# A two-layer transformer trunk with its own list scheduler: larger planned latencies for transfers and for TensorE's inputs, and all hi/lo splits on VectorE

## The chip, the cores and the metric

One NeuronCore of a Trainium2 chip runs the program alone. The metric is the device time of one execution in microseconds (us). Engine names are those of the profile: PE is TensorE's matmul row and PEld its weight loads, DVE is VectorE, ACT is ScalarE, POOL is GpSimd, and SP is SyncE, whose queue issues the DMAs.

## The reference, cut to what matters

The input is 512 tokens of 1024 float32 values. Two layers follow each other, and each has an attention part and a gated ConvFFN, both between an RMSNorm before and an RMSNorm after:

```python
for layer in range(2):
    if layer == 0:                        # stick-breaking attention
        a = rmsnorm(h, sb_pre_g[0])
        q, k, v = split(a @ sb_w_qkv[0], 3)
        o = stick_breaking_attention(q, k, v)       # 16 heads of 64
        h = h + rmsnorm(merge(o) @ sb_w_o[0], sb_post_g[0])
    else:                                 # forgetting attention
        kvf = rmsnorm(h, kv_norm_g) @ w_kvf         # keys, values, forget gates
        q = rmsnorm(h, fox_pre_g[0]) @ fox_w_q[0]
        o = forgetting_attention(q, k, v, fcum)
        h = h + rmsnorm(merge(o) @ fox_w_o[0], fox_post_g[0])
    hdn = causal_conv3(rmsnorm(h, ffn_pre_g[layer]) @ w_up[layer]) + conv_b
    gate, up = split(hdn, 2)              # 2816 columns each
    h = h + rmsnorm((gelu(gate) * up) @ w_down[layer], ffn_post_g[layer])
```

## The kernel before, in words

**Split operands.** Nearly every float32 matrix product is done with operands split in two: `hi` is the value rounded to the type that TensorE reads at full rate, and `lo` is what is left over. A product is then three matmuls, hi by hi, hi by lo and lo by hi. The activations are kept as `AH` and `AL` (hi and lo, 128 partitions by 8 by 512).

**Weights.** `stream` lists 196 weight tiles of 512 KB in the order of their use. `make` issues the transfer of a tile into `raw` (two buffers), casts it to `whi` on ACT (L389; with a per-row gain L382) and computes `wlo = raw - whi`, in two halves of 128x512 on the engine that the tile names (L393; with a gain L383, on DVE). `whi` and `wlo` have eight buffers each (`NW`). A `raw` buffer is free for the tile after next once both halves of `wlo` are done. The tile names DVE except for the rows 1, 5 and 7 of the two output projections (`sb_w_o`, `fox_w_o`), which name POOL (`POOL_ROWS`, L417 and L432).

**The phases.** "pre" loads and normalises the input and transposes small tables (tiles `crow` and `grow`, in two buffers, through PE at L885); tiles of a later phase reuse the memory of an earlier one, so the first write of the attention phase waits for the last use in "pre". Then come the attention of layer 0 (about 46 to 250 us of the span), its output projection and FFN (to about 660 us), and the same for layer 1. A head (`Attn.head`) is a chain over four engines: scores on PE (L643), exponentials on ACT and scans, masks and products on DVE (L653 to L681), transposes on PE (L689), a hi/lo split on ACT and DVE (L695, L696), the product with the values on PE (L701), and the merge (L710, L711). The projections of the next heads (L445 for q and k, L623 for v) and, late in the phase, the first output-projection matmuls (L743) stand between as work that PE can do while a head waits. At the end of `Attn.run` the attention's output is split too: `AH` by a cast on ACT (L730) and `AL` by a subtraction (L731), for the head pairs 0 to 3 on POOL and for 4 to 7 on DVE.

**The order is planned.** The class `Order` takes all instructions, works out who depends on whom, and simulates them at build time with costs written in the code (`cost`, `schedule`). At each step an engine takes, of the instructions whose inputs the plan says are there, the one of the lowest rank: the rank is the program position, plus 300 for weight casts and splits (`BEHIND`), less 150 for work that empties PSUM (`AHEAD`). The order that results is fixed for PE, DVE, ACT and POOL; SP's queue is not fixed by it. At run time the engines follow this order and wait at semaphores for true readiness. The plan's latencies decide only which instruction stands ahead of which. Of a transfer the plan holds that it lands `LEAD` + size/`BYTES` + `LAND` after its issue, 1300 + 1691 + 700 ns for 512 KB when the wire is free, and each result reaches another engine `HOP` = 60 ns after its end.

Of the kernel before, what the change touches and what calls it, by code (L numbers as in the profile page):

```python
# [18 lines left out]
KT = D // P  # L19
# [10 lines left out]
EARLY = 3  # L30
BEHIND = 300
AHEAD = 150
POOL_ROWS = (1, 5, 7)
FILL = (4, 5)
SCALE = HD**-0.5

# [4 lines left out]
def f32(ap):  # L41
    return ap.bitcast(F32)


class Order:
# [4 lines left out]

    GRAIN = 64
    SKIPPED = ("Drain", "EventSemaphore", "UnconditionalBranch", "TilePoolBoundary", "RegisterMove", "ISA", "Call")
    ISSUE, LEAD, LAND, BYTES = 520, 1300, 700, 310.0
    HOP = 60

    def __init__(self, tc, phases):
        self.tc, self.nc, self.phases = tc, tc.nc, phases
# [182 lines left out]
    def schedule(self, prog, preds):  # L240
        N = len(prog)
        rank = [n + self.shift.get(i.name, 0) - (AHEAD if self.evicts(i) else 0) for n, i in enumerate(prog)]
        eng = [self.engine(i) for i in prog]
        cost = [self.cost(i) for i in prog]
        succ = [[] for _ in range(N)]
        left = [len(d) for d in preds]
        for n, d in enumerate(preds):
            for m, k in d.items():
                succ[m].append((n, k))
        free = {e: 0.0 for e in sorted(set(eng))}  # L250
        now = {e: [] for e in free}
        later = {e: [] for e in free}
        at, start, wire = [0.0] * N, [0.0] * N, 0.0
        for n in range(N):
            if not left[n]:
                heapq.heappush(later[eng[n]], (0.0, n))
        for _ in range(N):
            best = None
            for e in free:
                if now[e]:  # L260
                    c = (free[e], e)
                elif later[e]:
                    c = (max(free[e], later[e][0][0]), e)
                else:
                    continue
                best = c if best is None else min(best, c)
            t, e = best
            while later[e] and later[e][0][0] <= t:
                m = heapq.heappop(later[e])[1]
                heapq.heappush(now[e], (rank[m], m))  # L270
            n = heapq.heappop(now[e])[1]
            hold, done = cost[n]
            start[n], free[e], end = t, t + hold, t + done
            if str(prog[n].opcode) == "DMACopy":
                wire = max(wire, t + self.LEAD) + done
                end = wire + self.LAND
            for m, k in succ[n]:
                at[m] = max(at[m], t if k == 2 else free[e] if eng[m] == e else end + self.HOP)
                left[m] -= 1
                if not left[m]:  # L280
                    heapq.heappush(later[eng[m]], (at[m], m))
        return start
# [3 lines left out]
def tile_trunk(  # L286
# [22 lines left out]
    nc = tc.nc  # L309
# [53 lines left out]
    stream = []  # L363
# [6 lines left out]
    def row_tile(w, k, eng=nc.vector):  # L370
        return (w[k * P : (k + 1) * P, :].rearrange("(a p) c -> p a c", p=P), 1, D, None, eng)
# [39 lines left out]
    for g in range(4):  # L411
        for pr in range(2):
# [1 line left out]
            qk = [col_tile(wq, c0), col_tile(wk, c0)]  # L414
            v = [col_tile(wv, g * 256, 256, 4 * j, 4) for j in range(2)]
            stream += qk if pr else qk + v if g else v + qk
    stream += [row_tile(sb_w_o[0], k, nc.gpsimd if k in POOL_ROWS else nc.vector) for k in range(KT)]  # L417

    def ffn_stream(l):
        s = []  # L420
        for c in range(NC):
            s += [col_tile(w_up[l], c * P), col_tile(w_up[l], FF + c * P)]
        return s + [row_tile(w_down[l], k) for k in range(NC)]

    stream += ffn_stream(0)
    for g in range(4):
        for pr in range(2):
# [1 line left out]
            qk = [col_tile(fox_w_q[0], c0, g=KT), col_tile(w_kvf, c0, g=0)]  # L429
            v = [col_tile(w_kvf, D + g * 256, 256, 4 * j, 4, g=0) for j in range(2)]  # L430
            stream += qk if pr else qk + v if g else v + qk
    stream += [row_tile(fox_w_o[0], k, nc.gpsimd if k in POOL_ROWS else nc.vector) for k in range(KT)]  # L432
    stream += ffn_stream(1)


# [69 lines left out]
    class Attn:  # L505
# [208 lines left out]
        def run(self):  # L714
            self.project_v(0, PAIRS)
            if self.fox:
                self.gates()
                self.project(0, 2, (PAIRS[1] + 1, PAIRS[2] + 1))
                self.gate_keys(0)
            else:  # L720
                self.project(0, 2, (PAIRS[0] + 1, PAIRS[1] + 1))
            for p in range(NPAIR):
                self.head(p, 0)
                if p + 1 < NPAIR:
                    self.project(p + 1)
                end = self.head(p, 1)
                if p % 2 and p + 1 < NPAIR:
                    self.project_v((p + 1) // 2)
            for p in range(NPAIR):
                nc.scalar.copy(AH[:, p, :], self.oT[:, p, :])  # L730
                (nc.gpsimd if p < 4 else nc.vector).tensor_tensor(  # L731
                    out=AL[:, p, :], in0=self.oT[:, p, :], in1=f32(AH[:, p, :]), op=ALU.subtract
                )
            return end
# [128 lines left out]
    with tc.tile_pool(name="pre", bufs=2) as pool:  # L863
# [13 lines left out]
        for l in range(2):  # L877
            rows = [conv_w[l, w].rearrange("(c p) -> c p", p=P) for w in range(3)]
            rows.append(conv_b[l].rearrange("(c p) -> c p", p=P))
            for i in range(2):  # L880
                t = pool.tile([2 * nb, P], F32, name="crow")
# [5 lines left out]
        t = pool.tile([2 * KT, P], F32, name="grow")  # L887
# [5 lines left out]
        t = pool.tile([P, NH], F32, name="bf")  # L893
# [14 lines left out]
    with tc.tile_pool(name="attn0", bufs=2) as pool:  # L908
        pool = order.pool(pool, "attn0", 2)
        act_table("natural_log_exp_and_others")  # L910
        end = Attn(pool, False).run()
# [3 lines left out]
    with tc.tile_pool(name="attn1", bufs=2) as pool:  # L915
        pool = order.pool(pool, "attn1", 2)
        act_table("natural_log_exp_and_others")
        end = Attn(pool, True).run()
# [28 lines left out]
```

## Time and profile before

| what | value |
|---|---|
| median of three runs | 1273.48 us (1272.51 to 1274.8) |
| the profiled execution | 1276.16 us |
| its span, first to last instruction | 1274.3 us |
| mean granted TensorE clock | 0.996 of full speed |
| busy | PE 97%, DVE 64%, ACT 51%, POOL 8% |

The profiled execution is one execution; its span leaves out 1.9 us at the two ends. PE's busy time counts a matmul's pipeline latency, so that a row of matmuls that each wait a little can still look busy.

### The profile page before, as it was taken

Reading aid. Unit: us, or ns where it says so; the run is one execution under the profiler, and the core shown is the slowest. Engines: PE = TensorE matmul, PEld = TensorE weight load, DVE = VectorE, ACT = ScalarE, POOL = GpSimd, SP = SyncE. Lnnn points to the kernel's source line nnn. Section 1 sums busy time; section 2 is a strip of 40 time slices with the busy share of each in tenths; the row PEclk is TensorE's granted clock in tenths of the full one; section 3 lists DMA queues with packets and bytes.
Section 4 is the critical chain, followed back from the end, with each engine's and each line's share of the span. In section 5 each row is a group of like instructions: output and inputs, shape, how many; then the busy total and the mean of one; then the engine's idle time right before and its main releaser. Section 6 shows DMA issues by size and latency. Waiting matters only on the chain.

```text
span 1274.3 us, 16774 instructions
## 1 busy us (share of the span) xinstructions
PE 1236.5 (97%) x6485; PEld 1054.5 (83%) x6485; DVE 815.1 (64%) x1304; ACT 650.8 (51%) x1085; POOL 101.0 (8%) x163
## 2 busy tenths in 40 slices
PE   6999999899999999999998999989999999999998
PEld 6788897689888888888897988867898888888886
DVE  5699989677655555433477988784675555554323
ACT  4678777555433333323577888774454333333221
POOL 2000003120000000000101221342100000000001
PEclk9999999999999999999999999999999999999999
DMA  5322221125433333333221122221443333333311
GB/s 188 108 75 83 68 67 50 50 83 149 114 92 93 98 100 99 100 96 90 63 78 41 50 65 69 65 85 50 121 144 100 100 99 99 94 93 96 99 33 66
DMA packets 145927, 111.97 MB, mean 88 GB/s; under 512 B 4680, under 2 KB 136120, under 8 KB 145848
## 3 DMA queue, kind: packets, MB, share of 16 engines
q1 hardware_dynamic: 145848, 110.90, 29.4%
q8 instruction: 51, 0.84, 0.3%
q14 instruction: 28, 0.23, 0.1%
HBM read 108.79 MB, written 2.10 MB: 87 GB/s over the span
## 4 chain that ended last, share of the span: by engine, by line
PE 80%; DVE 12%; ACT 3%; DMA 2%; POOL 1%; issue 1%; SPq 0%; DVEq 0%; POOLq 0%; ACTq 0%
PE PS L445 47%; PE PS L743 20%; PE PS L623 5%; PE PS L701 3%; PE PS L643 2%; DVE ec L679 2%; PE PS L689 2%; DVE wlo L393 1%; DVE ec L681 1%; DVE PL L696 1%; PE PS L466 1%; DVE t L463 1%; DMA H<-x_dram 1%; DVE H L477 1%; DVE QS L594 1%
## 5 line engine op out<-in xcount | busy, mean ns | idle before, releaser
L445 PE MATMUL PS<-AH,whi 128*128 128x512 f32 (+1 forms) x1088 | 398.7, 366 | 3.4 <-DVE QS L594 3.4
L445 PE MATMUL PS<-AL,whi 128*128 128x512 f32 (+1 forms) x1088 | 398.6, 366 | 0.0
L445 PE MATMUL PS<-AH,wlo 128*128 128x512 f32 (+1 forms) x1088 | 398.5, 366 | 0.0
L393 DVE TENSOR_TENSOR wlo<-raw,whi 128x512 fp32r<-128x512 f32 x332 | 219.0, 698 | 197.3 <-ACT whi L389 196.8
L389 ACT CAST whi<-raw 128x1024 fp32r<-128x1024 f32 x172 | 180.6, 1050 | 196.5 <-PE PS L445 171.8
L445 PEld LDWEIGHTS PS<-AH,whi 128*128 128x128 f32 x1088 | 206.1, 189 | 35.2 <-DVE QS L594 3.7
L445 PEld LDWEIGHTS PS<-AL,whi 128*128 128x128 f32 x1088 | 206.2, 190 | 31.7
L445 PEld LDWEIGHTS PS<-AH,wlo 128*128 128x128 f32 x1088 | 206.0, 189 | 31.8
L821 DVE SCALAR_TENSOR_TENSOR hc<-PS,cw,hc 128x511 f32<-128x511 f32 (+1 forms) x176 | 131.3, 746 | 5.9 <-ACT hc L819 2.9
L743 PE MATMUL PS<-whi,ah 128*128 128x512 f32 x352 | 109.2, 390 | 0.0
L743 PE MATMUL PS<-whi,al 128*128 128x512 f32 x352 | 109.1, 389 | 0.0
L743 PE MATMUL PS<-wlo,ah 128*128 128x512 f32 x352 | 109.0, 389 | 0.0
L844 DVE TENSOR_TENSOR al<-act,ah 128x512 fp32r<-128x512 f32 x44 | 30.3, 691 | 116.6 <-ACT ah L843 116.6
L843 ACT CAST ah<-act 128x512 fp32r<-128x512 f32 x44 | 27.4, 623 | 145.0 <-PE PS L743 138.1
L743 PEld LDWEIGHTS PS<-whi,al 128*128 128x128 f32 x352 | 66.1, 188 | 13.7
L743 PEld LDWEIGHTS PS<-wlo,ah 128*128 128x128 f32 x352 | 66.1, 188 | 13.7
L743 PEld LDWEIGHTS PS<-whi,ah 128*128 128x128 f32 x352 | 65.9, 188 | 13.6
L623 PE MATMUL PS<-whi,AH 128*128 128x256 f32 x256 | 73.9, 289 | 0.0
L623 PE MATMUL PS<-wlo,AH 128*128 128x256 f32 x256 | 73.6, 288 | 0.0
L623 PE MATMUL PS<-whi,AL 128*128 128x256 f32 x256 | 73.3, 287 | 0.0
L826 ACT ACTIVATE hc<-hc 128x512 f32<-128x512 f32 x44 | 27.8, 631 | 85.0 <-DVE hc L821 85.0
L451 POOL TENSOR_SCALAR ss<-ss 128x1 f32<-128x1 f32 x31 | 9.8, 315 | 771.1 <-ACT junk L474 720.1
(132 smaller groups left out, 1770.6 us busy)
## 6 DMA issues: line engine op xcount, KB each, us to landing
raw<-w_up_dram SPq DMA_DIRECT2D x88, 512.0 KB, 3.8
raw<-w_down_dram SPq DMA_DIRECT2D x44, 512.0 KB, 3.6
raw<-sb_w_qkv_dram SPq DMA_DIRECT2D x24, 512.0 KB, 3.8
raw<-w_kvf_dram SPq DMA_DIRECT2D x16, 512.0 KB, 3.7
raw<-sb_w_o_dram SPq DMA_DIRECT2D x8, 512.0 KB, 3.6
raw<-fox_w_q_dram SPq DMA_DIRECT2D x8, 512.0 KB, 3.7
raw<-fox_w_o_dram SPq DMA_DIRECT2D x8, 512.0 KB, 3.7
H<-x_dram SPq DMA_DIRECT2D x4, 512.0 KB, 8.3
```

The costliest lines, as they stand in the source:

```text
L389: order.move(nc.scalar.copy(hi, raw), BEHIND)
L393: order.move(eng.tensor_tensor(out=fl[:, s], in0=fr[:, s], in1=fh[:, s], op=ALU.subtract), BEHIND)
L445: nc.tensor.matmul(ps, a[:, k, :m], b[:, k, t0:t1], start=i == 0, stop=i == n - 1)
L623: nc.tensor.matmul(ps[:, o], a[:, k, sl], m[:, k % 4, :], start=i == 0, stop=i == 3 * KT - 1)
L643: nc.tensor.matmul(z[:, ZOFF[b] : ZOFF[b] + n], a[:, b * P : (b + 1) * P], m[:, :n], start=i == 0, stop=i == len(passes) - 1,)
L679: nc.vector.tensor_tensor_scan(C[:, ::-1], self.R[:, ::-1], C[:, ::-1], 0.0, ALU.mult, ALU.add)
L701: mm = nc.tensor.matmul(av[:, j * P :], V[:, j, hh, :], m[:, o : o + n], start=i == 0, stop=i == 7,)
L743: nc.tensor.matmul(y[:, c, :], s[:, sl], m[:, 0, c * 512 : (c + 1) * 512], start=k == 0 and i == 0, stop=k == n - 1 and i == 2,)
L821: nc.vector.scalar_tensor_tensor(out=hc[:, s:], in0=y[:, i, : T - s], scalar=col[:, 2 - s : 3 - s], in1=hc[:, s:], op0=ALU.mult, op1=ALU.add,)
L826: nc.scalar.activation(hs[0], hs[0], AF.Gelu_apprx_tanh)
L843: nc.scalar.copy(ah, act[:, k, :])
L844: nc.vector.tensor_tensor(out=al, in0=act[:, k, :], in1=f32(ah), op=ALU.subtract)
```

## The change

Three edits. `LAND`, the last part of a transfer's planned latency, goes from 700 to 2700 ns. `HOP` becomes 350 ns where the instruction that receives the result is one of PE, and stays at 60 ns for the other engines. And POOL loses its splits: the rows 1, 5 and 7 of both output projections (12 halves of 128x512) and `AL` of the head pairs 0 to 3 in both layers (8 subtractions of 128x512) go to DVE, as the other rows and pairs already did.

```diff
-POOL_ROWS = (1, 5, 7)
...
-    ISSUE, LEAD, LAND, BYTES = 520, 1300, 700, 310.0
-    HOP = 60
+    ISSUE, LEAD, LAND, BYTES = 520, 1300, 2700, 310.0
+
+    HOP = {"PE": 350}
...
             for m, k in succ[n]:
-                at[m] = max(at[m], t if k == 2 else free[e] if eng[m] == e else end + self.HOP)
+                at[m] = max(at[m], t if k == 2 else free[e] if eng[m] == e else end + self.HOP.get(eng[m], 60))
...
-    stream += [row_tile(sb_w_o[0], k, nc.gpsimd if k in POOL_ROWS else nc.vector) for k in range(KT)]
+    stream += [row_tile(sb_w_o[0], k) for k in range(KT)]
...
-    stream += [row_tile(fox_w_o[0], k, nc.gpsimd if k in POOL_ROWS else nc.vector) for k in range(KT)]
+    stream += [row_tile(fox_w_o[0], k) for k in range(KT)]
...
                 nc.scalar.copy(AH[:, p, :], self.oT[:, p, :])
-                (nc.gpsimd if p < 4 else nc.vector).tensor_tensor(
+                nc.vector.tensor_tensor(
                     out=AL[:, p, :], in0=self.oT[:, p, :], in1=f32(AH[:, p, :]), op=ALU.subtract
                 )
```

## Rows read from the trace of the kernel before

**Rows 1.** Busy time, share of the span and instructions of each engine.
```profile
PE 1236.5 (97%) x6485; PEld 1054.5 (83%) x6485; DVE 815.1 (64%) x1304; ACT 650.8 (51%) x1085; POOL 101.0 (8%) x163
```

**Rows 2.** Windows: length; busy of PE, PEld, DVE, ACT, POOL; PEclk; DMA share; GB/s.
```profile
0.00:46.00 46.00, 33.53 (x240) 31.66 (x241) 26.48 (x56) 21.62 (x33) 8.11 (x22) 1.00 0.53 165
46.00:186.00 140.00, 139.27 (x822) 121.37 (x821) 130.26 (x170) 106.02 (x142) 2.55 (x2) 0.99 0.27 80
186.00:250.00 64.00, 57.21 (x304) 46.12 (x303) 53.34 (x63) 42.67 (x61) 12.15 (x8) 1.00 0.12 39
...
276.00:660.00 384.00, 384.00 (x1920) 327.47 (x1919) 211.86 (x337) 161.96 (x244) 7.51 (x20) 1.00 0.34 98
...
830.00:880.00 50.00, 44.16 (x219) 34.66 (x219) 31.84 (x58) 31.63 (x67) 19.40 (x22) 1.00 0.24 75
```

**Rows 3.** Waits of the whole run: us in total, times, longest.
```profile
ACT whi L389 <- DMA raw<-w_up_dram: 16.5, 14, 3.1
...
ACT whi L389 <- DMA raw<-sb_w_qkv_dram: 5.7, 4, 3.1
...
PE PS L701 <- DVE PL L696: 3.1, 5, 1.4
...
PE PS L689 <- POOL ec L669: 2.3, 4, 1.0
...
PE PS L689 <- DVE ec L681: 1.9, 2, 1.2
```

**Rows 4.** Instructions that ran on POOL at L393.
```profile
L393 POOL TENSOR_TENSOR wlo<-raw,whi 128x512 fp32r<-128x512 f32 x12 | 15.9, 1346 | 205.5 <-ACT whi L389 205.5
```

**Rows 5.** Chain that ended last, 186 to 250 us: start, us, what.
```profile
196.25 1.66 DVE ec L653
197.91 1.29 DVE ec L655
...
204.41 2.75 DVE wlo L393 x2
...
219.51 0.56 DVE ec L653
220.07 0.20 DVE ec L655
220.27 0.60 DVE AL L731
...
246.57 2.52 POOL wlo L393 x2
```

**Rows 6.** POOL's timeline in the same stretch.
```profile
196.19 2.84 POOL L393 TENSOR_TENSOR wlo<-raw,whi 128x512 fp32r<-128x512 f32 x2 [33.26 <-ACT whi L389]
```

**Rows 7.** The same chain, 828 to 882 us.
```profile
848.39 1.13 DVE ec L669
...
850.93 2.26 DVE wlo L393 x2
...
856.90 0.49 DVE ec L669
```

**Rows 8.** The same chain, 24 to 60 us.
```profile
24.53 2.87 DMA crow<-conv_w_dram
...
34.64 1.20 DVE wlo L393 x2
...
36.70 6.57 DMA raw<-sb_w_qkv_dram
43.29 1.04 ACT whi L389
...
50.95 6.91 PE PS L445 x30
```

**Rows 9.** DMA issues: KB each, median us from issue to landing.
```profile
raw<-w_up_dram SPq DMA_DIRECT2D x88, 512.0 KB, 3.8
```

**Rows 10.** Windows around the first heads, columns as in Rows 2.
```profile
40.00:46.30 6.30, 4.03 (x23) 3.07 (x21) 3.20 (x5) 2.35 (x4) 0.00 (x0) 1.00 0.34 104
46.30:49.70 3.40, 3.31 (x9) 2.63 (x9) 1.91 (x4) 2.11 (x3) 0.00 (x0) 0.50 0.48 154
```

## The prediction

> **What bounds the kernel now.** I read the busy times first: PE is busy 97% of the span and no other engine more than 64% [rows 1], so only what lies between PE's matmuls can be won. The windows by stage say where that is [rows 2]. In the FFN of layer 0 (276 to 660 us) PE is busy all 384.00 of 384 us: an edit that acts there alone is worth nothing. PE's idle time sits at the start (46.00 - 33.53 = 12.5 us) and in the last heads of the two attention phases, 64.00 - 57.21 = 6.8 us in one and 50.00 - 44.16 = 5.8 us in the other. The same rows give the second engine to watch: DVE is busy 130.26 of 140 us in most of the first attention phase and 53.34 of 64 us at its end, but only 31.84 of 50 us at the end of the second.
>
> The waits come next [rows 3]. ACT stands 16.5 us for transfers of `w_up`, all of it under the FFNs, where PE does not notice; 5.7 us for `sb_w_qkv`, at the start. PE's own waits for a head's results are short: 3.1 + 2.3 + 1.9 = 7.3 us in 11 waits. Last I read the chain that ended last, in the stretches with idle PE. In 186 to 250 us it goes mostly through DVE, and some of its DVE steps are far longer than the same step elsewhere [rows 5]: L653 takes 1.66 us and later 0.56, L655 1.29 and later 0.20, two halves of `wlo` 2.75 us where the two at 34.64 took 1.20 [rows 8]. POOL was subtracting `wlo` when L653 and L655 were slow, from 196.19 for 2.84 us [rows 6].
>
> **The change, part by part.**
>
> *Splits from POOL to DVE.* Gone are 12 halves on POOL [rows 4] and 8 subtractions for `AL`, four a layer. What they cost on the chain: 1.66 - 0.56 = 1.10, 1.29 - 0.20 = 1.09 and 2.75 - 1.20 = 1.55 us of slowed DVE work, and the last pair of halves that PE's first output block waits for, 2.52 us on POOL where DVE has 1.20: 1.32 us. That is 5.06 us in layer 0 [rows 5, 8]. In layer 1 it is 1.13 - 0.49 = 0.64 and 2.26 - 1.20 = 1.06, together 1.70 us [rows 7]. So 6.8 us can be given back. Added on DVE are 20 instructions; half of a pair is 0.60 us [rows 8], and one `AL` was 0.60 us [rows 5]. The pair at 246.57 is already netted, so 18 x 0.60 = 10.8 us are new. Their cover is DVE's idle time, 64.00 - 53.34 = 10.7 us and 50.00 - 31.84 = 18.2 us [rows 2]; queued behind each new split is the next step of a head, and PE's transposes or value products behind that. Splits have the lowest priority in the plan, so I expect them in gaps, but an instruction that has begun is finished: I let a bit under half of their time, 4.5 us, reach the chain. Net: 4.5 - 6.8 = -2.3 us. Bounds: -6.8 us (all in gaps) and 10.8 - 6.8 = +4.0 us (none).
>
> One rule speaks against this edit. DVE is the busier engine by the rows, 815.1 us against POOL's 101.0 [rows 1]. The Trainium skill, "Perfetto Trace Analysis", section "Optimizing Scalar/DVE Operations", says that when DVE is saturated, handing some elementwise work to GpSimd may make sense, and adds that the two share a read port, so it might not help. By its first half this part of the sum would be the +4.0, by its second half the -6.8; the slow L653 beside POOL's `wlo` agrees with the second.
>
> *`HOP` 350 for PE.* The plan now thinks that each result reaches PE 290 ns later, so PE takes another ready matmul first, and at run time the result is there when its turn comes. What it can save is bounded by the 7.3 us of waits in 11 places [rows 3]. 11 x 0.29 = 3.2 us would go if each were shortened by the margin and a filler stood ready; late in a phase fillers run out, so I take -2.5 us. The price is a filler ahead of a result that was in time: 6.91 / 30 = 0.23 us for an L445 matmul [rows 8]. A head enters PE three times (scores, transposes, value products). If, an estimate, the last four heads of each layer have no slack and every entry is hit, that is 2 x 4 x 3 x 0.23 = 5.5 us. Bounds: -7.3 us (all waits gone) and +5.5 us.
>
> *`LAND` 2700.* The plan's old latency for 512 KB, 3.69 us, is close to the measured median of 3.8 [rows 9]. With 5.69 us the casts stand later in ACT's order. In the FFNs this removes some of the 16.5 us and moves nothing, since PE is full. It matters at the start. There a transfer took 6.57 us (36.70 to 43.27), ACT then cast it for 1.04 us with the key copies of the first head queued behind, PE was idle for 6.30 - 4.03 = 2.3 us, and after that idle time the granted clock was 0.50, the 1.2 GHz level, for 3.4 us [rows 8, 10], a loss of 1.7 us. With the copies ahead of the cast, 1.04 us and perhaps the clock's 1.7 us are won: -2.7 us. Against it: the plan's start is transfers in series. The `crow` tables come in two rounds, the second issued when the first has passed PE; each round is planned 2 us later, PE keeps the transposes back accordingly, and the whole attention phase waits for the last of them (the 2.87 us `crow` transfer is on the chain [rows 8]). That is up to +4.0 us. I see no reason for either sign and take 0.
>
> SP issues the same transfers, so nothing is added to its queue. Sum: -2.3 - 2.5 + 0 = -4.8 us. Against the profiled execution (span 1274.3, 1276.16 with its ends) that is 1271.4; the profiled execution is 2.7 us above the median of the runs, so for the median it is 1273.5 - 4.8 = 1268.7 us.
>
> **The rivals.**
>
> *DVE becomes the bound in the attention phases (slower).* For it: in 46 to 186 us DVE has only 9.7 us idle in 140 and the chain at 186 to 250 is DVE's. Against it: nearly all of the moved work falls after 186 us, where idle DVE time is larger than the work. It decides if more than 6.8 of the 10.8 us reach the chain; all of it gives 1273.5 + 4.0 = 1277.5 us if `HOP` then finds nothing to win. This is where the skill's advice on a saturated DVE would lead.
>
> *The margin on transfers delays the start (slower).* Two planned rounds of `crow`, +4.0 us, and as much again at the two hand-overs from output projection to FFN, where two `raw` buffers feed six tiles in a row: 1273.5 + 8.0 - 4.8 = 1276.7 us. Against it: PE is busy 384 of 384 us just behind the first hand-over [rows 2]. It decides when the loss is over 4.8 + 2.5 = 7.3 us.
>
> *The waits come back elsewhere (same).* PE's fillers are finite: what is filled in earlier is missing in the last heads, where PE already idles 6.8 and 5.8 us. Then `HOP` nets nothing and the splits alone remain: 1273.5 - 2.3 = 1271.2 us.
>
> **How the numbers follow.** A measurement of this kernel can tell about 0.2%, 2.5 us, from no change. I give the forecast 0.54, the waits that come back 0.20, DVE as the bound 0.16, and the delayed start 0.10. The first lies below 1270.9 us, the second within 0.2%, the last two above 1276.0: faster 0.54, same 0.20, slower 0.26. For the range the three terms are taken as independent. The distances to their good ends are 4.5, 4.8 and 2.7 us, whose squares add to 7.1 us; to their bad ends 6.3, 8.0 and 4.0 us, which give 10.9 us. That is 1261.6 to 1279.6, rounded to 1261 and 1280 us: the low end leaves out little, the high end takes in both slower rivals. Within the forecast alone I expect 1262 to 1270.9.
>
> **What would show it.** Splits: L653, L655 and `wlo` in the last heads of layer 0 at their short times, POOL without L393 and L731, DVE's idle time at 186 to 250 us smaller, and PE's too. `HOP`: PE's waits on L696, L681 and L669 below 7.3 us. `LAND`: ACT's waits for `w_up` far below 16.5 us without effect on the FFNs' length; the key copies stand ahead of the cast and the half clock after them is gone, or the `crow` transfer of the chain lands later than 27.4 us. The prediction is wrong if the attention phases get longer although the collisions are gone (DVE), if the start does, or if the plan's new order opens a wait that none of these rows shows: then the size and perhaps the sign is set by that.

## The result, and the profile after

The changed kernel takes 1261.97 us (median of four executions, 1261.11 to 1262.29) against 1272.99 us before: a ratio of 0.9900, 95% interval 0.9875 to 0.9925. That is 11.0 us less where 4.8 us less was forecast, and at the low end of the range. Its profiled execution took 1261.11 us, with a span of 1259.4 us.

The engines' busy times, as in [rows 1]:

```profile
PE 1230.2 (98%) x6485; PEld 1055.0 (84%) x6485; DVE 820.4 (65%) x1324; ACT 649.1 (52%) x1085; POOL 72.8 (6%) x143
```

POOL has 20 instructions less and DVE 20 more, as the edit says. PE runs the same 6485 matmuls but is *busy* 6.3 us less (1236.5 - 1230.2). A busy time that falls with the work unchanged means that part of it was waiting, or time at half clock.

The windows by stage, columns as in [rows 2]:

```profile
0.00:46.00 46.00, 36.61 (x256) 35.19 (x257) 26.32 (x55) 21.92 (x35) 8.04 (x22) 1.00 0.49 153
46.00:186.00 140.00, 139.55 (x852) 123.72 (x852) 134.88 (x177) 108.40 (x146) 0.00 (x0) 1.00 0.25 76
186.00:250.00 64.00, 58.85 (x288) 46.35 (x286) 54.35 (x71) 43.16 (x61) 2.47 (x5) 1.00 0.21 66
...
276.00:660.00 384.00, 384.00 (x1923) 327.59 (x1922) 210.50 (x345) 164.07 (x254) 6.12 (x16) 1.00 0.33 97
...
830.00:880.00 50.00, 46.16 (x231) 37.81 (x232) 33.85 (x58) 27.81 (x60) 9.56 (x19) 1.00 0.18 62
```

The FFN of layer 0 is as full as before; PE's idle time shrank where it was: 9.4 us at the start (12.5 before), 5.2 us at the end of the first attention phase (6.8) and 3.8 us at the end of the second (5.8). DVE has more to do and is still not full.

The waits, as in [rows 3]:

```profile
ACT whi L389 <- DMA raw<-w_up_dram: 10.6, 8, 3.1
...
PE PS L701 <- DVE PL L696: 2.8, 4, 1.5
PE PS L689 <- DVE ec L681: 2.0, 3, 1.0
...
PE PS L689 <- POOL ec L669: 1.2, 2, 1.0
```

ACT's wait for `w_up` fell from 16.5 to 10.6 us, without effect on the FFN. But PE's waits for a head's results, on which the forecast of `HOP` rested, only fell from 7.3 to 6.0 us. Most of the gain must be elsewhere.

The chain that ended last, 186 to 250 us, as in [rows 5]:

```profile
191.44 1.20 DVE wlo L393 x2
...
205.19 0.56 DVE ec L653
...
222.91 0.56 DVE ec L653
223.47 0.20 DVE ec L655
```

L653, L655 and the pairs of `wlo` have their short times; POOL does nothing there until 243.81 us. ACT's timeline at the start of the heads:

```profile
40.60 0.58 ACT L603 CAST KH<-PS 64x512 fp32r<-64x512 f32 x1 [1.83 <-PE PS L445]
41.20 0.58 ACT L604 CAST KH<-PS 64x512 fp32r<-64x512 f32 x1
...
43.61 1.04 ACT L389 CAST whi<-raw 128x1024 fp32r<-128x1024 f32 x1
```

The key copies now stand ahead of the cast, and the half clock near 46 us is gone. The first score matmul starts at 42.24 us (45.58 before), that of the second head at 52.67 us (57.68).

### The profile page after: what moved, and what is told of

The parts are those of the page before. It is cut to its first block, busy times and chain, and to the rows that moved or that the text cites. A ratio compares the mean times of both kernels' runs of the same rounds, so it can differ in the third digit from the quotient of the medians.

```text
span 1259.4 us, 16728 instructions
## 1 busy us (share of the span) xinstructions
PE 1230.2 (98%) x6485; PEld 1055.0 (84%) x6485; DVE 820.4 (65%) x1324; ACT 649.1 (52%) x1085; POOL 72.8 (6%) x143
## 4 chain that ended last, share of the span: by engine, by line
PE 83%; DVE 13%; ACT 2%; issue 2%; DMA 0%; POOL 0%; SPq 0%; DVEq 0%; POOLq 0%; ACTq 0%
PE PS L445 48%; PE PS L743 24%; PE PS L623 5%; DVE ec L679 2%; DVE wlo L393 2%; PE PS L701 2%; DVE PL L696 2%; PE PS L643 1%; PE PS L689 1%; DVE ec L681 1%; PE PS L466 1%; DVE QS L594 1%; DVE KL L605 1%; DVE oT L711 1%; DVE ec L676 1%
## 5 line engine op out<-in xcount | busy, mean ns | idle before, releaser
L393 DVE TENSOR_TENSOR wlo<-raw,whi 128x512 fp32r<-128x512 f32 x344 | 222.8, 687 | 166.2 <-ACT whi L389 165.5
L445 PEld LDWEIGHTS PS<-AL,whi 128*128 128x128 f32 x1088 | 205.8, 189 | 31.3
L819 ACT ACTIVATE hc<-PS,cw 128x512 f32<-128x512 f32 x88 | 68.4, 777 | 36.0 <-PE PS L445 36.0
L743 PEld LDWEIGHTS PS<-whi,al 128*128 128x128 f32 x352 | 66.1, 188 | 13.7
L743 PEld LDWEIGHTS PS<-whi,ah 128*128 128x128 f32 x352 | 66.0, 188 | 13.6
```

The lines of the kernel that those rows point to most:

```text
L393: order.move(eng.tensor_tensor(out=fl[:, s], in0=fr[:, s], in1=fh[:, s], op=ALU.subtract), BEHIND)
L445: nc.tensor.matmul(ps, a[:, k, :m], b[:, k, t0:t1], start=i == 0, stop=i == n - 1)
L743: nc.tensor.matmul(y[:, c, :], s[:, sl], m[:, 0, c * 512 : (c + 1) * 512], start=k == 0 and i == 0, stop=k == n - 1 and i == 2,)
L819: nc.scalar.activation(hc, y[:, i, :], AF.Identity, scale=col[:, 2:3], bias=col[:, 3:4])
```

## The experiments

Theory A: the margin for PE is the gain, and it removes more of PE's waiting than the named waits of the heads. Rival B: the start is the gain, by `LAND`. Rival C: the splits. Rival D: any other planned order would do as well, so it is luck. The letters in the quoted expectations are those of each expectation and stand for other theories. Each kernel's ratio is against the kernel before, run on the same chip (medians 1272.27 to 1275.20 us).

### The three edits, alone and in pairs

**e1_land**, the margin on transfers alone:

```diff
-    ISSUE, LEAD, LAND, BYTES = 520, 1300, 700, 310.0
+    ISSUE, LEAD, LAND, BYTES = 520, 1300, 2700, 310.0
```

> LAND 2700 alone, HOP and the splits as before. Theory A (the gains are local: each edit repairs the place that its rows name): the start is LAND's, because the first head's scores began 3.3 us earlier in the changed kernel and the half clock behind them is gone; so about -5 us, 1268 us, with the first score near 42 us and nothing gained after the first attention phase. Theory B (the start is HOP's, PE's order being what changed there): 1273 us within 2, first score near 45 us. Theory C (any change of the plan's latencies reshuffles all engines and the sum is luck): a time anywhere between 1264 and 1277, with changes of both signs in stages that have no transfer waits.

Measured: 1274.74 us, ratio 1.000 (0.9987 to 1.0013). As an account of the measured gain rival B falls, and oddly: its second head starts at 52.57 us, as early as in the changed kernel, and the down projection of layer 0 at 513.10 us against 519.18 before, but nothing is left of it at the end.

**e2_hop**, the margin for PE alone:

```diff
-    HOP = 60
+    HOP = {"PE": 350}
...
+                at[m] = max(at[m], t if k == 2 else free[e] if eng[m] == e else end + self.HOP.get(eng[m], 60))
```

> HOP 350 for PE alone. Theory A: only the small waits of heads, -3 us, 1270 us, the start unchanged (first score near 45.5 us). Theory B: -5 to -8 us, 1266 us, with the start repaired (first score near 42 us, no half clock near 46 us). Theory C: between 1264 and 1277, stages changing with both signs.

Measured: 1263.93 us, ratio 0.9912 (0.9894 to 0.9930): nearly the whole gain, and nearest to theory B of its expectation: the half clock near 46 us is gone, and the first score matmul starts at 43.87 us.

**e3_splits**, the splits alone:

```diff
-POOL_ROWS = (1, 5, 7)
...
+    stream += [row_tile(sb_w_o[0], k) for k in range(KT)]
...
+    stream += [row_tile(fox_w_o[0], k) for k in range(KT)]
...
-                (nc.gpsimd if p < 4 else nc.vector).tensor_tensor(
+                nc.vector.tensor_tensor(
```

> All splits on DVE alone, LAND and HOP as before. Theory A: the two output projections, which ended 2.4 and 2.0 us earlier in the changed kernel than the attention before them explains, are due to this edit: -4 us, 1269 us; the start is unchanged to 0.3 us. Rival (DVE is too full without the margins): +1 to +4 us, 1275 us, the attention phases longer by the added 10.8 us less the 6.8 us of slowed work. Theory C as above.

Measured: 1274.02 us, ratio 1.0001 (0.9985 to 1.0017). Rival C falls too, for the time as measured.

**e4_land_hop**, the first two together:

```diff
+    ISSUE, LEAD, LAND, BYTES = 520, 1300, 2700, 310.0
+    HOP = {"PE": 350}
...
```

> LAND and HOP together, the splits of 12 weight halves and 8 subtractions still on POOL. Theory A: -11 us less the splits' 4, so -7 us, 1266 us, and the sum of the first two experiments within 1.5 us. Theory C: the sum of the two singles misses it by more than 3 us.

Measured: 1269.01 us, ratio 0.9954 (0.9936 to 0.9971), 5 us worse than `HOP` without `LAND`. **e5_land_splits**, the whole change without `HOP`:

```diff
+    ISSUE, LEAD, LAND, BYTES = 520, 1300, 2700, 310.0
     HOP = 60
...
+                nc.vector.tensor_tensor(
```

> LAND 2700 and the splits on DVE, HOP at 60. Each of the two alone left the time where it was, with long half-clock stretches near 681 and 855 us in both profiles. Theory H (HOP is what pays, and the other two only matter beside it): 1274 us within 3, half-clock stretches after PE's idle times at the end of the attention phases as before. Theory A (gains of the stages add): LAND's 5 us at the start and the splits' 2.7 us at the first output projection are both there, so 1268 us or less.

Measured: 1273.36 us, ratio 0.9976 (0.9959 to 0.9994). **e6_hop_splits**, the whole change without `LAND`:

```diff
     ISSUE, LEAD, LAND, BYTES = 520, 1300, 700, 310.0
+    HOP = {"PE": 350}
...
+                nc.vector.tensor_tensor(
```

> HOP 350 and the splits on DVE, LAND at 700. Theory H: HOP's 9.9 us stay and the splits add their output projections, 1260 to 1264 us, faster than or equal to the whole change. Theory I (LAND is needed with the splits, since HOP and LAND alone gave only 4.8 us and the whole change 11): 1266 to 1271 us.

Measured: 1264.36 us, ratio 0.9907 (0.9883 to 0.9931). The times of the three edits don't add up in any simple way; the clock, below, tells a part of why.

### Which part of the margin

**e7_hop_data** gives 350 ns only to values that PE reads. A set of pairs (writer, reader) is kept while the dependences are found:

```diff
+            self.data |= {(wrote[g], n) for g in gr if g in wrote and g[0] not in self.banks}
...
-                at[m] = max(at[m], t if k == 2 else free[e] if eng[m] == e else end + self.HOP)
+                at[m] = max(at[m], t if k == 2 else free[e] if eng[m] == e else end + (350 if eng[m] == "PE" and (n, m) in self.data else self.HOP))
```

> Of HOP's 350 ns only the part for values that PE reads from SBUF (weights, activations, scores to be transposed); the release of a PSUM bank to PE stays at 60 ns. Theory D (the margin pays because an operand that is there early lets the weight load run under the matmul before): nearly all of HOP's gain, 1263 to 1266 us, and the small waits of the weight loads on L696, L681 and L669 shrink. Theory E (it pays because PE no longer stands before a bank that VectorE or ScalarE has still to empty): 1272 us within 2.

**e8_hop_bank** gives it only to the rest, the PSUM banks that come free for PE:

```diff
+                at[m] = max(at[m], t if k == 2 else free[e] if eng[m] == e else end + (350 if eng[m] == "PE" and (n, m) not in self.data else self.HOP))
```

> The other part alone: 350 ns for the release of PSUM banks to PE, 60 ns for values. Theory D: 1273 us within 2. Theory E: 1263 to 1266 us, with the wait of L445 for L594 (3.0 us near 685 us) and that of L743 for L663 gone.

Measured: e7 1262.60 us, 0.9897 (0.9872 to 0.9922), against e8 1272.16 us, 0.9978 (0.9961 to 0.9996). It is the data, for all that the time shows; the banks alone give at most a few us.

**e11_hop_heads** gives it only to the matmuls of a head, whose names are collected at L643, L689 and L701:

```diff
+                at[m] = max(at[m], t if k == 2 else free[e] if eng[m] == e else end + (350 if eng[m] == "PE" and prog[m].name in self.of_head else self.HOP))
```

> 350 ns only for the matmuls of the heads (L643, L689, L701); projections, output and down matmuls at 60 ns. Theory P (the prediction's place: results of a head that PE waits for): nearly all of the 9.9 us, 1263 to 1266 us. Theory Q (the weights and activations of the projections, which fill between the heads, are what came late): 1272 us within 2.

**e12_hop_rest** gives it to PE's other matmuls (`not in self.of_head`):

```diff
+                at[m] = max(at[m], t if k == 2 else free[e] if eng[m] == e else end + (350 if eng[m] == "PE" and prog[m].name not in self.of_head else self.HOP))
```

> The other matmuls alone: 350 ns for L445, L623, L743 and the transposes of the norms, 60 ns for the heads. Theory P: 1272 us within 2. Theory Q: 1263 to 1266 us. If the two halves share it, about 1269 us each.

Measured: e11 1268.73 us, 0.9954 (0.9938 to 0.9969), and e12 1271.40 us, 0.9973 (0.9956 to 0.9989). The heads have the greater part, and the projections some of their own.

### How much, and for whom

**e9_hop_120**, **e14_hop_240** and **e13_hop_700** change the number of e2, in this order:

```diff
+    HOP = {"PE": 120}
...
+    HOP = {"PE": 240}
...
+    HOP = {"PE": 700}
```

> HOP 120 ns for PE instead of 350, nothing else changed. A pair's weight load takes about 190 ns and one L445 matmul 230. Theory D (a result has to be there a weight load and a matmul before its turn): 60 ns more cover neither, so little is won, 1270 to 1274 us. Theory F (the plan only has to know that results never come early, any margin will do): most of HOP's gain, 1263 to 1267 us.

> HOP 240 ns for PE. 120 won nothing and 350 won 9.9 us. Theory G: 240 is a weight load (190 ns) and little more, so part of the gain, 1266 to 1271 us. If the step lies at one L445 matmul (230 ns): most of the gain, 1264 us. Theory C: anywhere.

> HOP 700 ns for PE, nothing else changed. Theory G (a size that has to be reached, some 350 ns, and more costs little because PE has fillers): 1262 to 1266 us as with 350. Theory K (a peak: with more, fillers stand ahead of results that are in time and the heads' chains get longer, 12 handovers a head by 0.35 us): 1268 us or more. Theory C (luck): anywhere from 1262 to 1277.

**e10_hop_others** gives 350 ns to all engines but PE, **e15_hop_all** to all:

```diff
+                at[m] = max(at[m], t if k == 2 else free[e] if eng[m] == e else end + (60 if eng[m] == "PE" else 350))
...
+    HOP = 350
```

> The margin with its engines exchanged: 350 ns into VectorE, ScalarE, GpSimd and the transfers, 60 ns into PE. Theory D (PE's inputs alone pay): 1273 us within 3. Theory F (slack anywhere makes the order robust): some 5 us faster, 1268 us. Theory C (luck of a new order): anywhere between 1262 and 1277.

> HOP 350 ns into all engines. Into PE alone it won 9.9 us, into all others alone 5.5. If the two repair different places: 1259 to 1261 us, faster than the whole change. If they repair the same places (PE's short waits, by an earlier result or by a later turn): 1263 to 1266 us.

Measured: e9 1274.83 us, 0.9998 (0.9981 to 1.0015); e14 1266.52 us, 0.9950 (0.9938 to 0.9963); e13 1264.65 us, 0.9942 (0.9929 to 0.9954). As measured, a margin of 120 ns does nothing that can be told, 240 ns does more than half, and twice the 350 ns does no more. e10 gives 1268.50 us, 0.9949 (0.9932 to 0.9966), and e15 1266.13 us, 0.9948 (0.9934 to 0.9961): the two margins save much of the same time.

### Is it luck of one order?

**e16_hop_bytes** and **e18_hop_bytes2** are e2 with another planned rate of transfers (in this order), which reshuffles the order. Counted by operand names and shapes in the traces, e16 has another matmul than e2 at 1501 of PE's 6485 places, the kernel before at 1383; e18 at 774, so it is the milder test.

```diff
+    ISSUE, LEAD, LAND, BYTES = 520, 1300, 700, 300.0
...
+    ISSUE, LEAD, LAND, BYTES = 520, 1300, 700, 320.0
```

> HOP 350 into PE as in the second experiment, and the planned transfer rate 300 instead of 310, which moves 57 ns per weight tile in the plan: about as many lines of PE's order differ as between 60 and 350 ns, with no reason for a gain or a loss. Theory G: the gain stays within 3 us, 1261 to 1267 us. Theory C: anywhere from 1262 to 1277.

> The margin of 350 ns alone, with the planned rate of transfers at 320 in place of 310, a second reshuffle of the order. If the margin itself saves some 6 to 11 us and the order adds luck of 2 to 3 us, 1262 to 1267 us, ratio 0.991 to 0.996. If the gain was mostly one lucky order, 1270 or more, ratio 0.998 to 1.001.

Measured: e16 1266.26 us, 0.9950 (0.9937 to 0.9962), and e18 1263.92 us, 0.9905 (0.9877 to 0.9932). Rival D falls: three orders with the margin alone lie in 1263.9 to 1266.3 us (with `LAND` beside it, e4, it was 1269.0). The orders with at most 120 ns for PE's data and 60 ns for the other engines (e1, e3, e5, e8, e9 and the kernel before) lie in 1272.2 to 1275.2 us.

**e17_all_data** is the whole change with the margin for data only:

```diff
-    HOP = {"PE": 350}
+    HOP = 60
...
+                at[m] = max(at[m], t if k == 2 else free[e] if eng[m] == e else end + (350 if eng[m] == "PE" and (n, m) in self.data else self.HOP))
```

> The whole change, with the 350 ns only for values that TensorE reads from SBUF and 60 ns for PSUM banks that come free. If the data half is all of the gain, as alone, 1262 to 1265 us, ratio 0.989 to 0.9925, not to be told from the changed kernel. If the bank half has a price beside the other edits, below 1260. If the whole change needs both halves, 1266 or more.

Measured: 1266.63 us, 0.9926 (0.9901 to 0.9950). By its expectation the whole change would need both halves; the clock, next, is enough to account for the difference, so that is not shown. None of the variants is clearly faster than the changed kernel, and by their ratios e2, e6, e7 and e18 cannot be told from it.

### The clock under all of them

Each trace gives the span and the mean granted clock (1 is 2.4 GHz, 0.50 is 1.2 GHz, "half clock"). The kernel before:

```profile
core 0: 1274.3 us, clock 0.996
```

e2:

```profile
core 0: 1260.2 us, clock 0.999
```

The changed kernel:

```profile
core 0: 1259.4 us, clock 0.997
```

e17:

```profile
core 0: 1265.7 us, clock 0.991
```

e17 is slower than the changed kernel by 6.3 us, and here is where. Windows of e17 at the stretches of half clock and just ahead of each (PE's busy time is the second number, PEclk the third from the end):

```profile
214.90:218.50 3.60, 1.97 (x11) 1.04 (x9) 3.60 (x2) 1.84 (x3) 0.00 (x0) 1.00 0.00 0
218.50:225.30 6.80, 5.56 (x21) 4.66 (x21) 6.38 (x11) 4.50 (x7) 0.00 (x0) 0.50 0.00 0
675.70:679.30 3.60, 1.43 (x8) 0.96 (x6) 2.96 (x6) 3.42 (x7) 0.74 (x2) 1.00 0.36 108
679.30:686.10 6.80, 5.65 (x13) 4.51 (x14) 5.19 (x12) 5.97 (x19) 1.64 (x3) 0.50 0.00 0
833.00:836.30 3.30, 1.91 (x9) 1.29 (x9) 3.21 (x8) 3.12 (x6) 0.00 (x0) 1.00 0.00 0
836.30:839.70 3.40, 3.40 (x10) 2.63 (x9) 3.40 (x7) 2.88 (x8) 0.00 (x0) 0.50 0.42 154
850.00:853.40 3.40, 1.45 (x10) 0.89 (x8) 3.31 (x7) 1.47 (x4) 1.64 (x3) 1.00 0.53 154
853.40:856.80 3.40, 3.23 (x9) 2.65 (x10) 1.99 (x5) 2.35 (x9) 0.00 (x0) 0.50 0.03 7
```

Each stretch at 1.2 GHz comes just behind one in which PE was idle for 1.4 to 2.2 us; together they last 20.4 us, which costs up to half of it, 10.2 us: in the full half-clock stretch of the kernel before (688.00 us, below) the interval from one 512-column matmul to the next is 0.43 us where 0.23 is usual. The changed kernel has one such stretch between its first and last matmul:

```profile
676.00:679.40 3.40, 0.68 (x3) 0.59 (x4) 3.13 (x7) 3.22 (x8) 0.00 (x0) 1.00 0.00 0
679.40:682.80 3.40, 3.40 (x10) 2.63 (x9) 3.10 (x9) 3.30 (x13) 0.48 (x1) 0.50 0.00 0
```

That is up to 1.7 us. e2 has none, although at the same place it idles too (windows of e2):

```profile
679.40:682.80 3.40, 1.87 (x10) 1.65 (x11) 2.54 (x7) 2.97 (x10) 0.00 (x0) 1.00 0.38 111
```

Between e17 and the changed kernel the difference of up to 8.5 us covers the 6.3, so the clock alone can account for it. Which of the two orders is quicker at full clock is not shown (e17 is 0.8 us longer in the table below).

The kernel before and e1 differ in the same way. The kernel before has half clock at 46.30 us [rows 10] and here:

```profile
688.00:691.40 3.40, 3.40 (x8) 2.65 (x9) 2.88 (x8) 3.27 (x12) 0.00 (x0) 0.51 0.00 0
```

In e1 (`LAND` alone) the first of the two is gone, and three stretches stand later:

```profile
219.90:223.30 3.40, 3.27 (x15) 2.96 (x14) 3.10 (x4) 2.18 (x4) 0.00 (x0) 0.50 0.00 0
680.70:687.50 6.80, 5.09 (x12) 4.08 (x13) 5.75 (x13) 6.40 (x20) 1.50 (x3) 0.50 0.00 0
854.80:861.60 6.80, 5.32 (x17) 3.64 (x17) 3.98 (x9) 2.98 (x8) 2.19 (x3) 0.50 0.30 89
```

That is 17.0 us against 6.8, up to 5.1 us more lost; 6.1 us ahead at the down projection of layer 0, e1 ends its span only 2.4 us ahead.

Every execution's mean granted clock can be used the same way. Time x clock is an estimate of the time that it would have taken at full clock; the rest of its time is the most that half clock can have cost (0.5 to 2.6 us of that, by the traces, is a stretch at the end, behind the last matmul, where it costs PE nothing). Means over all executions, 98 of the kernel before and 4 to 12 of each other:

| kernel | mean clock | time x clock, us | rest, us |
|---|---|---|---|
| before (98 executions) | 0.9961 | 1269.9 | 4.9 |
| e1 `LAND` | 0.9919 | 1264.3 | 10.3 |
| e2 `HOP` | 0.9977 | 1260.3 | 2.9 |
| e3 splits | 0.9942 | 1267.2 | 7.4 |
| e4 `LAND` + `HOP` | 0.9920 | 1258.7 | 10.2 |
| e5 `LAND` + splits | 0.9920 | 1263.1 | 10.2 |
| e6 `HOP` + splits | 0.9955 | 1258.5 | 5.7 |
| all three | 0.9955 | 1256.2 | 5.7 |
| e17 all three, data only | 0.9923 | 1257.0 | 9.7 |
| e7 data | 0.9968 | 1258.9 | 4.0 |
| e8 banks | 0.9950 | 1266.0 | 6.4 |
| e9 120 ns | 0.9939 | 1267.1 | 7.8 |
| e10 other engines | 0.9944 | 1261.2 | 7.1 |
| e11 heads | 0.9965 | 1264.5 | 4.4 |
| e12 rest of PE | 0.9957 | 1265.9 | 5.5 |
| e13 700 ns | 0.9978 | 1262.5 | 2.8 |
| e14 240 ns | 0.9972 | 1262.8 | 3.5 |
| e15 all engines | 0.9954 | 1260.6 | 5.8 |
| e16 other order of e2 | 0.9960 | 1261.2 | 5.1 |
| e18 other order of e2 | 0.9962 | 1259.4 | 4.8 |

In the third column all three edits gain: `LAND` 5.6 us, `HOP` 9.6 us, the splits 2.7 us; the three together gain 13.7 us, less than the sum of 17.9. The three orders of e2 agree within 2 us, and the gain grows with the margin, without a sharp step: 60, 120, 240, 350 ns give 1269.9, 1267.1, 1262.8 and about 1260.3 us. The ten kernels with 350 ns or more for all of PE's data lie at 1256.2 to 1262.5 us, the six with at most 120 ns for it and 60 ns for the other engines at 1263.1 to 1269.9. `LAND` and the splits alone lose in half clock what they gained.

The product overstates the gain of a kernel that ran at a lower mean clock. Within the 98 executions of the kernel before, 0.001 of mean clock goes with 0.97 us, where the product takes off 1.27. Read from a line through those 98 executions, that is at an equal mean clock, `LAND` gains 4.3 us, `HOP` 10.1, the splits 2.0 and the three together 13.6. Added to the other edits, the splits gain 1.2 to 2.5 us in the third column, so their sign holds and their size is near the error.

A check that needs neither: the 18 executions of the kernel before at a mean clock of 0.999 have a median of 1271.4 us; two of e2 at the same 0.999 took 1261.65 and 1261.88 us.

## Why the prediction was right or wrong

**The failed step: the term for `HOP` was mis-sized.** It took -2.5 us and held that what the margin "can save is bounded by the 7.3 us of waits in 11 places". Alone it saves some 10 us (9.9 as measured, 9.6 by the third column). The waits of PE in e2, the three of the bound and two others:

```profile
PE PS L701 <- DVE PL L696: 4.0, 7, 1.3
PE PS L445 <- DVE QS L594: 1.5, 1, 1.5
...
PE PS L689 <- DVE ec L681: 1.1, 2, 0.6
...
PE PS L643 <- ACT KH L604: 1.0, 1, 1.0
PE PS L689 <- POOL ec L669: 0.8, 1, 0.8
```

The bounded waits lost only 1.4 us (7.3 to 5.9). All rows of this view together lost 7.0 us (31.0 to 24.0), so 5.6 us went in rows that the bound left out. In the kernel before, the largest of them for heads and projections are:

```profile
PE PS L445 <- DVE QS L594: 3.4, 2, 3.0
...
PE PS L643 <- ACT KH L604: 2.3, 1, 2.3
...
PE PS L643 <- ACT ec L663: 1.6, 1, 1.6
PE PS L643 <- DVE QS L594: 1.2, 1, 1.2
```

The 3.0 us stand at 684.9 us, ahead of the second attention phase, a place that the prediction's list of idle times does not have; half clock followed there at 688.00 us. In e2 that wait is 1.5 us and no half clock follows. And half of the difference between the two traces is in no row of waits. From the busy times of e2:

```profile
PE 1229.4 (98%) x6485; PEld 1052.9 (84%) x6485; DVE 813.5 (65%) x1304; ACT 650.6 (52%) x1085; POOL 98.5 (8%) x163
```

the span fell by 14.1 us (1274.3 to 1260.2; the profiled execution of the kernel before was longer than its median, that of e2 shorter), of which 7.1 us is busy time of PE (1236.5 - 1229.4, the same 6485 matmuls) and 7.0 us idle time. The kernel before had two stretches of half clock, 3.4 us each, and e2 none between its first and last matmul: that is up to 3.4 us of the 7.1. The intervals from one matmul's start to the next say the same, each set against its usual length (the median before of the same operands and shape):

| excess over the usual interval | before, us (places) | e2, us (places) |
|---|---|---|
| in half clock | 3.5 (17) | 0 |
| more than 0.35 us, at full clock | 26.8 (27) | 20.6 (25) |
| 0.04 to 0.35 us, at full clock | 19.6 (203) | 17.2 (192) |

The last row holds the short waits that a busy share hides. They fell by only 2.4 us, and in e7, which gained as much as e2, they are 19.3 us, so they are not shown to carry the gain. The rest of the 7.1 us, some 1 to 2 us, was not taken apart. So the bound failed in two ways: it took three rows for all of PE's waiting, and it had no term for half clock behind the waits. The Trainium skill ("Perfetto Trace Analysis", "Identifying the Most-Contended Engine") advises to judge TensorE's headroom by its useful work per time and the busy share of its weight loads, and not by the busy share of its matmuls; here that share of the weight loads was 83% [rows 1] where the matmuls' was 97%, and it rose to 84% in e2. The bound also counted only the entries of heads, whereas the runs show margins paying at the other matmuls (e12) and at other engines (e10).

**The price of `HOP`** (fillers ahead of results that were in time, up to 5.5 us) does not show at 350 ns in any of three orders; 700 ns, at 1262.5 us against 1259.4 to 1261.2 of those three in the third column, may pay a little of it.

**The splits:** -2.3 us was forecast; at full clock they gave an estimated -2.0 to -2.7. That is the forecast size, and the first half of the mechanism is there: in e3, the splits alone, none of the steps of L653 and L655 (there one line up) at 186 to 250 us is slow any more, and the down projection of layer 0 starts at 516.50 us against 519.18, behind one equal stretch of half clock in each. How much of the new DVE time reached the chain was not measured. On the clock as it was granted the edit alone is worth nothing, which no term of the sum foresaw. Of the two halves of the skill's rule on handing elementwise work to GpSimd (the Trainium skill, "Perfetto Trace Analysis", "Optimizing Scalar/DVE Operations"), these runs fit the second: bringing the work back did not slow the kernel, with DVE at 65%. That the port is the reason no run here shows.

**`LAND`:** 0 was forecast and 1.000 was measured, but not for want of an effect. Each part that was seen is there: the key copies ahead of the cast and no half clock behind them; `crow` later (its last transpose, L885, at 31.3 us against 28.6, in the changed kernel), which the heads did not mind. At full clock that is an estimated -4.3 to -5.6 us, beyond the bound of -2.7; half clock elsewhere takes about as much back. That the term of 0 came out was luck.

**The rivals.** DVE did not become the bound, the start was not delayed, and the waits did not come back elsewhere, though the last came nearest: for `LAND` and the splits alone something did come back, as half clock and not as a wait.

**The range** (1261 to 1280) held the time at its low end, which owed more to the width of the good bounds than to the argument: `HOP` alone, at 9.9 us, went past the 7.3 us that its own bound allowed.

**What stays open.** Which idle gaps end in half clock differs from order to order without a cause in the edits that could be shown, and decides up to some 5 us. That PE takes up a value by a weight load and a matmul, each of some 0.2 us, so that a margin of 60 ns always comes one place too late, was only argued, and the gain that grows from 120 to 350 ns without a sharp step does not decide it. Why margins for the other engines alone save as much as 8.7 us at full clock, and add nothing to PE's, was not taken apart; it may be that slack in the plan helps wherever it is put in.

## What to carry to other kernels

Where a list scheduler takes a result as ready a few tens of ns after its end, try a larger margin on the inputs of the bound engine before finer costs: here 350 ns, more than one matmul's length, saved some 10 us, where 120 ns saved nothing that could be measured. Bound such an edit by all the time between an engine's instructions, start to start, and not by a few named waits: the busy time of an engine at 97% fell by as much as its idle time, half of that by half clock. Compare variants at equal mean clock as well as by median, since an order that is better between its stalls can lose its gain to half clock behind them, as `LAND` alone did here.

## What the runs showed of the hardware that was not expected

The spread of executions of one kernel goes with the clock. The kernel before took from 1270.38 us at a mean granted clock of 0.999 to 1281.51 us at 0.990; over 98 executions the correlation of time and clock is -0.97, and time x clock averages 1269.9 us with a standard deviation of 1.2, where that of the time is 2.9. In the 20 traces the level falls from 2.4 to 1.2 GHz just behind gaps between PE's matmuls that add up to 1.2 to 3.0 us, and shows 1.2 GHz for 3.4, 6.8 or 10.2 us even where PE is busy for nearly all of that time. Gaps of that size do not always bring it: e13 idled for 1.8 us behind 681.0 us, e2 for 1.5 us behind 679.4 us, and both went on at 2.4 GHz. An idle stretch of 2 us that is followed by 3.4 us at half clock so costs up to 3.7 us, an estimate from these lengths.
